# Retention's scores of two token tiles in one stretch, with the delays of TensorE's order set anew

## The chip, the core and the metric

The kernel runs on one core of a Trainium2 chip. The core has five engines that work side by side: TensorE (PE; its weight loads are listed as PEld), VectorE (DVE), ScalarE (ACT), GpSimd (POOL) and SyncE (SP), and queues of DMA transfers. Each engine takes its own instructions in order and waits on semaphores for the others. TensorE writes into PSUM, here eight banks; the other engines read from there. The metric is the time of one execution in microseconds (us), the median over several.

## What is computed

Two layers, each over 1024 tokens of width 1024, with three groups of heads side by side: sliding-window attention (A), retention (B) and gated linear attention, GLA (C). The reference, cut to what matters here:

```python
mod = c_act @ w_mod + b_mod
shift, scale, gate = jnp.split(mod[:, None, :], 3, axis=-1)
h = rms_norm(x, pre_gain) * (1.0 + scale) + shift
proj = h @ w_in                     # columns: aq ak av ag | rq rk rv rg | gq gk gv gg ga
...
r = retention(rq, rk, rv)           # after a rotation of rq and rk
r_out = rms_norm(r) * jax.nn.silu(rg)
...
y = jnp.concatenate([a_out, r_out, g_out], axis=-1) @ w_out
return x + gate * rms_norm(y, post_gain)
```

Retention goes over eight chunks of 128 tokens, four heads of width 64:

```python
def step(state, inp):
    qi, ki, vi = inp
    sc = jnp.einsum('bhid,bhjd->bhij', qi, ki) * dmask
    intra = jnp.einsum('bhij,bhjv->bhiv', sc, vi)
    inter = jnp.einsum('bhid,bhdv->bhiv', qi * q_decay, state)
    new_state = chunk_decay * state + jnp.einsum('bhjd,bhjv->bhdv', ki * k_decay, vi)
    return new_state, intra + inter
```

The state goes from chunk to chunk; the scores `sc` of a chunk need no state.

## The kernel before

**Tiles and projections.** A token tile is 128 tokens, so there are eight tiles and four pairs of them. A projection of one tile to 256 columns is 24 products on TensorE (`accum`, the helper's line L161): eight slices of the width, in three passes, since weights and inputs are split in a high and a low part (L478 makes the low one, L145 and L147 the high one). Retention loops over the pairs: for each of rq, rk and rv it projects the even tile, then the odd one, each into one of three banks `mm`. DVE rotates q and k (L692 to L698) and multiplies them by the decay (L1050) into buffers of the small ring `t1`, which has eight; ACT copies v (L145) into the same ring. The other five banks are `aux`.

**A retention tile.** `ret_core` does for a tile: four transpositions of q and k (L176) into one bank and their copy by ACT (L145); four score products into two banks, one for each half of the 128 rows that a head of width 64 takes; two masks by DVE (L1072); the output's products `po`, for which the state `stR` must be ready; the state's products `pst` and its update by DVE (L1091, L1093). Then come the gate's load (a DMA issued by ACT) and the head norm (L863 to L869). A product of the scores has a shape of 64x128 in the profile and stands there as two instructions.

**What sets the order.** TensorE's order is fixed by the program: code is written out in the order in which TensorE runs it. A planner keeps a clock `clk`, to which each product adds an assumed cost. Everything but the projections is a job, a generator that yields a delay from the table `L` (by `lat(key, l)`; a key ending in `@1` holds for layer 1) or a flag that it must await. Each seven products of a projection `pump` lets those jobs run whose time has come by the planner's clock. So the delays, not the semaphores, say behind which product a transposition or a score stands. The instructions of the other engines are ordered by a scheduler that follows from this, and buffers and banks go round in rings: who asks for the next one waits until the oldest is read.

```python
    def pump():
        moved = True
        while moved:
            moved = False
            for j in list(jobs):
                r = ready(j)
                if r is not None and r <= clk[0]:
                    step(j)
```

**Other places that the table moves.** At the front, input tiles are normalised, transposed (16 transpositions for two tiles, released by DVE's L544, the reader of TensorE being the projection of the tile), split by ACT (L577) and POOL (L581). In the modulation, DVE sums the rows of `w_mod` (L361), TensorE transposes the row and DVE copies it (L273). GLA's scores are 112 small products of a 32x128 shape for each pair of tiles, behind decays by DVE and ACT (L995). L892 takes the GLA gate's projection out of its bank, L807 and L812 are attention's softmax, L1018 writes GLA's masked scores.

## Time and profile before

| | |
|---|---|
| median of 3 runs | 1021.76 us (1021.18 to 1021.92) |
| the profiled execution | 1022.61 us |
| its span in the trace | 1020.9 us |
| mean granted clock of TensorE | 0.978 |
| instructions of TensorE in the trace | 7185 |

The profile's page lists the busy time of each engine as a share of the span, then the span in 40 equal slices, where a digit is the busy share in tenths and the row PEclk is the clock that TensorE was granted, in tenths of full speed. The chain is the work that ended last, followed back from the end: at each step to what released it. A row of the order of time reads: start, duration, engine, line, operation, output<-input, shape, count, and in brackets the idle time ahead of it with its releaser. Rows of one kind that follow each other are put together, so that the start is the first one's. Matmuls overlap, so the time that a product takes is read from the distance between starts. A row of a window reads: the stretch, its length, busy time and count of PE, PEld, DVE, ACT and POOL, the clock, the DMA share and the GB/s.

The layers take about half the span each: retention of layer 0 lies at 110 to 210, GLA's scores of layer 0 at 250 to 370, retention of layer 1 at 600 to 700, GLA's of layer 1 from 718.

### The profile page before, as it was taken

Reading aid. Unit: us, or ns where it says so; the run is one execution under the profiler, and the core shown is the slowest. Engines: PE = TensorE matmul, PEld = TensorE weight load, DVE = VectorE, ACT = ScalarE, POOL = GpSimd, SP = SyncE. Lnnn points to the kernel's source line nnn. Section 1 sums busy time; section 2 is a strip of 40 time slices with the busy share of each in tenths; the row PEclk is TensorE's granted clock in tenths of the full one; section 3 lists DMA queues with packets and bytes.
Section 4 is the critical chain, followed back from the end, with each engine's and each line's share of the span. In section 5 each row is a group of like instructions: output and inputs, shape, how many; then the busy total and the mean of one; then the engine's idle time right before and its main releaser. Section 6 shows DMA issues by size and latency. Waiting matters only on the chain.

```text
span 1020.9 us, 19368 instructions
## 1 busy us (share of the span) xinstructions
PE 975.0 (96%) x7185; PEld 845.1 (83%) x7185; DVE 652.3 (64%) x1565; ACT 377.2 (37%) x1050; POOL 284.5 (28%) x310
## 2 busy tenths in 40 slices
PE   5899999999999999999999999999999999999997
PEld 1588899888998777777888999988899887777886
DVE  3699856766757688754477486676575566763322
ACT  2466321322321556631354342123232256562111
POOL 2343101423331154520235120133243224542000
PEclk8899999999899999999999999999998999999999
DMA  8941613423334245768636142234032214455653
GB/s 292 309 129 47 182 57 104 131 86 109 91 94 141 74 124 164 244 190 268 218 134 202 48 147 71 60 114 138 22 105 86 94 51 134 148 153 185 227 185 144
DMA packets 124153, 140.44 MB, mean 138 GB/s; under 512 B 12462, under 2 KB 95384, under 8 KB 124060
## 3 DMA queue, kind: packets, MB, share of 16 engines
q1 hardware_dynamic: 116060, 127.50, 40.3%
q10 hardware_dynamic: 8000, 11.72, 3.2%
q8 instruction: 56, 0.92, 0.4%
q14 instruction: 37, 0.30, 0.1%
HBM read 102.48 MB, written 34.60 MB: 134 GB/s over the span
## 4 chain that ended last, share of the span: by engine, by line
PE 67%; DVE 13%; DMA 7%; issue 4%; ACT 3%; POOL 1%; SPq 1%; DVEq 0%; POOLq 0%; ACTq 0%
PE mm L161 52%; PE aux L161 11%; PE aux L176 4%; DMA st<-in_w_mod_dram 3%; DVE arena L478 1%; DVE acc L361 1%; DMA t<-t 1%; POOL sm L514 1%; DVE t L573 1%; ACT smx L812 1%; SPq L150 1%; DMA st<-in_w_out_dram 1%; DMA mx<-mixS 1%; DVE t L1050 1%; DVE smx L807 0%
## 5 line engine op out<-in xcount | busy, mean ns | idle before, releaser
L161 PE MATMUL mm<-arena 128*128 128x256 f32 (+2 forms) x1824 | 298.2, 319 | 5.4 <-ACT arena L577 3.0
L161 PE MATMUL mm<-arena,arena 128*128 128x256 f32 (+2 forms) x1824 | 294.3, 318 | 5.0 <-ACT sm L892 2.5
L161 PEld LDWEIGHTS mm<-arena 128*128 128x128 f32 x1824 | 258.5, 193 | 27.3 <-ACT arena L577 3.2
L161 PEld LDWEIGHTS mm<-arena,arena 128*128 128x128 f32 x1824 | 257.3, 192 | 28.2 <-ACT sm L892 3.0
L161 PE MATMUL mm<-arena,mx 128*128 128x512 f32 (+1 forms) x816 | 180.2, 380 | 0.1
L161 PEld LDWEIGHTS mm<-arena,mx 128*128 128x128 f32 x816 | 146.0, 188 | 30.4 <-issue 1.2
L514 POOL TENSOR_TENSOR sm<-sm,mhalf 128x1 f32<-128x1 f32 (+1 forms) x64 | 54.2, 847 | 324.7 <-DVE sm L513 311.8
L478 POOL TENSOR_TENSOR arena<-st,arena 128x512 fp32r<-128x512 f32 x66 | 96.3, 1470 | 94.9 <-ACT arena L145 72.1
L145 ACT ACTIVATE t<-aux 128x512 f32<-128x512 f32 (+1 forms) x96 | 49.2, 522 | 114.3 <-PE aux L176 49.5
L816 POOL TENSOR_TENSOR smx<-smx,sm 128x512 f32<-128x512 f32 x32 | 35.2, 1100 | 112.9 <-DVE sm L815 109.1
L478 DVE TENSOR_TENSOR arena<-st,arena 128x512 fp32r<-128x512 f32 x62 | 60.5, 987 | 7.3 <-ACT arena L145 5.4
L361 DVE SCALAR_TENSOR_TENSOR acc<-st,c_act,acc 128x512 f32<-128x512 f32 x60 | 48.0, 799 | 23.1 <-DMA st<-in_w_mod_dram 22.5
L145 ACT ACTIVATE arena<-st 128x512 fp32r<-128x512 f32 x90 | 52.3, 624 | 20.5 <-PE mm L161 10.9
L812 ACT ACTIVATE smx<-smx,sm 128x129 f32<-128x129 f32 x128 | 50.0, 394 | 20.9 <-DVE sm L809 20.9
L176 PE MATMUL aux<-c_ident,t 128*128 128x128 f32 x288 | 47.2, 288 | 8.0 <-DVE t L544 4.1
L1105 ACT ACTIVATE t<-mm 128x512 f32<-128x512 f32 x30 | 17.9, 596 | 95.8 <-PE mm L161 45.8
L1106 DVE TENSOR_TENSOR t<-mm,modg 128x512 f32<-128x512 f32 x30 | 20.7, 689 | 49.8 <-ACT t L1105 48.6
L176 PEld LDWEIGHTS aux<-c_ident,t 128*128 128x128 f32 x288 | 34.9, 146 | 14.5 <-DVE t L544 5.9
L161 PEld LDWEIGHTS aux<-t,mx 32*128 32x128 f32 (+1 forms) x896 | 43.0, 200 | 4.5 <-DVE sm L273 1.4
L161 PE MATMUL aux<-t,mx 32*128 32x32 f32 (+1 forms) x896 | 44.2, 283 | 2.1 <-DVE sm L273 1.3
L1141 DVE SCALAR_TENSOR_TENSOR t<-t,sm,t 128x512 f32<-128x512 f32 x32 | 23.3, 752 | 35.2 <-DMA t<-xs 19.3
L863 ACT ACTIVATE t<-aux 128x256 f32<-128x256 f32 x32 | 12.3, 384 | 73.8 <-PE aux L161 65.1
(191 smaller groups left out, 1243.0 us busy)
## 6 DMA issues: line engine op xcount, KB each, us to landing
st<-in_w_in_dram SPq DMA_DIRECT2D x96, 256.0 KB, 3.7
st<-in_w_mod_dram SPq DMA_DIRECT2D x64, 256.0 KB, 2.6
mx<-mixS SPq DMA_DIRECT2D x32, 512.0 KB, 5.4
mixS<-t SPq DMA_DIRECT2D x64, 128.0 KB, 2.5
st<-in_w_out_dram SPq DMA_DIRECT2D x32, 256.0 KB, 3.1
mixS<-t SPq DMA_DIRECT2D x32, 256.0 KB, 2.4
wm<-in_w_mod_dram SPq DMA_DIRECT2D x12, 512.0 KB, 7.2
t<-in_x_dram SPq DMA_DIRECT2D x24, 256.0 KB, 4.6
```

The costliest lines, as they stand in the source:

```text
L145: A.activation(dst, src, AF.Copy)
L161: T.matmul(dst, lhsT, rhs, start=start, stop=stop)
L176: T.transpose(dst, src, idn)
L361: V.scalar_tensor_tensor(acc, wt, c_act[:, k:k + 1], acc, ALU.mult, ALU.add)
L478: (G if first == 0 else eng(f"wlo{kc}")).tensor_tensor(wt[:, 1, 2 * kc:2 * kc + 2, 0:256], st, f(hi), ALU.subtract)
L514: G.tensor_tensor(r, r, mhalf[:, :w], ALU.pow)
L812: A.activation(sm[:, h, :], sm[:, h, :], AF.Exp, bias=mx[:, h:h + 1], accum_out=sums[:, h:h + 1])
L816: eng("pn").tensor_tensor(sm[:, :, 0:128], sm[:, :, 0:128], rs.unsqueeze(2).to_broadcast((P, 4, P)), ALU.mult)
L863: A.activation(sq, po, AF.Square)
L1105: A.activation(yg, pm, AF.Square, accum_out=ss[:, nh:nh + 1])
L1106: V.tensor_tensor(yg, pm, modg[l][:, 512 * nh:512 * nh + 512], ALU.mult)
L1141: V.scalar_tensor_tensor(xt[j], yg[j], r, xt[j], ALU.mult, ALU.add)
```

## The change

`ret_core` is taken apart. `ret_turn`, a job for each tile, makes the transpositions and their copy. `ret_core` is now one job for a pair: it starts when both tiles are turned and both have their v, makes the eight score products of the two tiles in one stretch, into the same two banks (tile i in columns 256 i on), then the four masks (L1081 in the changed file), and then for each tile the output's products, the state's products and the state's update (L1102, L1104). `ret_out`, again a job for each tile, loads the gate and does the head norm. Each of the eight products costs the planner 0.112 us where one cost 0.213 by its default. The table `L` has new values nearly throughout. The number of instructions stays the same on TensorE; each kind of work is there as often as before.

```diff
@@ -1050,51 +1050,65 @@
         eng("rdec").tensor_tensor(h4(r), h4(r), dec_.unsqueeze(2).to_broadcast((P, 4, 64)), ALU.mult)
         return r
 
-    def ret_core(l, t, q, k, v):
+    def ret_turn(l, t, q, k):
         yield lat("rc1", l)
         pt = aux()
         for j in range(2):
             transp(pt[:, j * P:(j + 1) * P], q[:, j * P:(j + 1) * P], ident)
             transp(pt[:, (2 + j) * P:(3 + j) * P], k[:, j * P:(j + 1) * P], ident)
         tt_ = t2()
-        qT = tt_[:, 0:256]
-        kTt = tt_[:, 256:512]
         copy("rT", tt_, pt)
-        yield lat("rc2", l)
+        turned[(l, t)] = tt_
+        flag(("rT", l, t), lat("rc2", l))
+
+    turned = {}
+
+    def ret_core(l, p, ks, vs):
+        ts = (2 * p, 2 * p + 1)
+        for t in ts:
+            yield (0.0, ("rT", l, t))
+        qT = [turned[(l, t)][:, 0:256] for t in ts]
+        kT = [turned[(l, t)][:, 256:512] for t in ts]
         sp = [aux(), aux()]
-        for h in range(4):
-            r = slice(64 * (h % 2), 64 * (h % 2) + 64)
-            c = slice((h // 2) * P, (h // 2) * P + P)
-            mult(sp[h % 2][:, c], kTt[r, c], qT[r, c], True, True)
-        sc = t2()
-        scv = h4(sc)
-        for c in range(2):
-            V.tensor_tensor(scv[:, c:4:2], sp[c][:, 0:256].rearrange("p (h q) -> p h q", h=2),
-                            causal.unsqueeze(1).to_broadcast((P, 2, P)), ALU.mult)
+        for i in range(2):
+            for h in range(4):
+                r = slice(64 * (h % 2), 64 * (h % 2) + 64)
+                c = slice((h // 2) * P, (h // 2) * P + P)
+                mult(sp[h % 2][:, 256 * i + c.start:256 * i + c.stop], kT[i][r, c], qT[i][r, c], True, True, 0.112)
+        sc = [t2(), t2()]
+        for i in range(2):
+            for c in range(2):
+                V.tensor_tensor(h4(sc[i])[:, c:4:2], sp[c][:, 256 * i:256 * i + 256].rearrange("p (h q) -> p h q", h=2),
+                                causal.unsqueeze(1).to_broadcast((P, 2, P)), ALU.mult)
         yield lat("rc3", l)
-        if t > 0:
-            yield (0.0, ("stR", l, t))
-        po = aux()
-        for j in range(2):
+        for i, t in enumerate(ts):
             if t > 0:
-                mult(po[:, j * P:(j + 1) * P], qT[:, j * P:(j + 1) * P], stR[:, j, :], True, False)
-            for h in (2 * j, 2 * j + 1):
-                mult(po[:, 64 * h:64 * h + 64], sc[:, h * P:(h + 1) * P], v[:, 64 * h:64 * h + 64],
-                     t == 0, t == 0 or h % 2 == 1)
-        if t < NT - 1:
-            pst = aux()
+                yield (0.0, ("stR", l, t))
+            po = aux()
             for j in range(2):
-                mult(pst[:, j * P:(j + 1) * P], k[:, j * P:(j + 1) * P], v[:, j * P:(j + 1) * P], True, True)
-            for c in range(2):
-                r = slice(64 * c, 64 * c + 64)
-                blk = stR[r, :, 64 * c:64 * c + 64]
-                V.tensor_tensor(blk, blk, pst[r, 0:256].rearrange("p (j n) -> p j n", j=2)[:, :, 64 * c:64 * c + 64],
-                                ALU.add)
-            V.tensor_tensor(stR, stR, cdt.unsqueeze(2).to_broadcast((P, 2, P)), ALU.mult)
-            flag(("stR", l, t + 1), lat("rc4", l))
+                if t > 0:
+                    mult(po[:, j * P:(j + 1) * P], qT[i][:, j * P:(j + 1) * P], stR[:, j, :], True, False)
+                for h in (2 * j, 2 * j + 1):
+                    mult(po[:, 64 * h:64 * h + 64], sc[i][:, h * P:(h + 1) * P], vs[i][:, 64 * h:64 * h + 64],
+                         t == 0, t == 0 or h % 2 == 1)
+            if t < NT - 1:
+                pst = aux()
+                for j in range(2):
+                    mult(pst[:, j * P:(j + 1) * P], ks[i][:, j * P:(j + 1) * P], vs[i][:, j * P:(j + 1) * P],
+                         True, True)
+                for c in range(2):
+                    r = slice(64 * c, 64 * c + 64)
+                    blk = stR[r, :, 64 * c:64 * c + 64]
+                    V.tensor_tensor(blk, blk, pst[r, 0:256].rearrange("p (j n) -> p j n", j=2)[:, :, 64 * c:64 * c + 64],
+                                    ALU.add)
+                V.tensor_tensor(stR, stR, cdt.unsqueeze(2).to_broadcast((P, 2, P)), ALU.mult)
+                flag(("stR", l, t + 1), lat("rc4", l))
+            job(ret_out(l, t, po[:, 0:256]))
+
+    def ret_out(l, t, po):
         sg = t1()
         dma("lsr", sg, srS[t])
-        yield from head_norm_gate(l, t, po[:, 0:256], sg, 4.0 / 64.0, 4.0 * EPS, 4)
+        yield from head_norm_gate(l, t, po, sg, 4.0 / 64.0, 4.0 * EPS, 4)
 
 
     def y_half(l, t, nh, mixt, ss, yg):
@@ -1203,7 +1217,10 @@
                     if name == "rv":
                         v = t1()
                         copy("rv", v, src)
-                        job(ret_core(l, t, rr[("rq", tt)], rr[("rk", tt)], v))
+                        rr[("rv", tt)] = v
+                        job(ret_turn(l, t, rr[("rq", tt)], rr[("rk", tt)]))
+                        if tt:
+                            job(ret_core(l, p, [rr[("rk", i)] for i in range(2)], [rr[("rv", i)] for i in range(2)]))
                     else:
                         rr[(name, tt)] = ret_rot(t, src, qdec if name == "rq" else kdec)
                     pump()
...
-"rc1": 0.8, "rc2": 1.47, "rc3": 1.99, "rc4": 2.79, "fin1": 10.74, "lay1": 1.23,
+"rc1": 0.05, "rc2": 1.52, "rc3": 1.31, "rc4": 2.31, "fin1": 7.77, "lay1": 1.23,
...
```

What the table does to the order is seen in four places. In the rows the number behind a name tells one buffer from another, and differs between the two kernels for the same thing. The first is TensorE at the front, with the projections of tiles 0 and 1 (`mm_410` to `mm_556`) and tile 2's first product (`mm_617` before, `mm_614` now). Before:

```order
L161 MATMUL mm_410<-arena_71 128x272 x24
L161 MATMUL mm_444<-arena_71 128x272 x21
L176 MATMUL aux_466<-c_ident,t_53_319 128x128 x4
L176 MATMUL aux_478<-c_ident,t_54_320 128x128 x4
L176 MATMUL aux_490<-c_ident,t_58_331 128x128 x4
L176 MATMUL aux_502<-c_ident,t_59_332 128x128 x4
L161 MATMUL mm_444<-arena_71 128x272 x3
L161 MATMUL mm_526<-arena_318,arena_71 128x256 x24
L161 MATMUL mm_556<-arena_318,arena_71 128x256 x24
L176 MATMUL aux_598<-c_ident,sm_442 16x128
L161 MATMUL mm_617<-arena_71 128x272 x24
```

and now:

```order
L161 MATMUL mm_410<-arena_71 128x272 x24
L161 MATMUL mm_444<-arena_71 128x272 x24
L161 MATMUL mm_478<-arena_318,arena_71 128x256 x24
L161 MATMUL mm_508<-arena_318,arena_71 128x256 x7
L176 MATMUL aux_516<-c_ident,t_53_319 128x128 x4
L176 MATMUL aux_528<-c_ident,t_54_320 128x128 x4
L176 MATMUL aux_540<-c_ident,t_58_331 128x128 x4
L176 MATMUL aux_552<-c_ident,t_59_332 128x128 x4
L161 MATMUL mm_508<-arena_318,arena_71 128x256 x17
L176 MATMUL aux_615<-c_ident,sm_442 16x128
L161 MATMUL mm_614<-arena_71 128x272 x24
```

The 16 transpositions of tiles 2 and 3 have moved behind 34 more products; between them and tile 2's first product there were 51, and are 17.

The second is TensorE at the last pair of retention in layer 0: transpositions, then score products (`aux`<-`t` of 128x128, alternating between two banks), then the output's products, which read `stR`. Of rows that repeat in turn only the first ones are shown. Before (the even tile's):

```order
L161 MATMUL mm_2404<-arena_318 128x256 x7
...
L176 MATMUL aux_2424<-c_ident,t_389_2194 128x128
L176 MATMUL aux_2424<-c_ident,t_409_2306 128x128
...
L161 MATMUL mm_2404<-arena_318 128x256 x14
L161 MATMUL aux_2445<-t_432_2429 128x128
L161 MATMUL aux_2446<-t_432_2429 128x128
...
L161 MATMUL mm_2404<-arena_318 128x256 x3
L161 MATMUL mm_2480<-arena_71,arena_318 128x512 x4
...
L161 MATMUL aux_2499<-stR,t_432_2429 128x128
```

and now (the odd tile's transpositions, the scores of both tiles, the even tile's output):

```order
L161 MATMUL mm_2465<-arena_71,arena_318 128x512 x4
L176 MATMUL aux_2470<-c_ident,t_387_2222 128x128
L176 MATMUL aux_2470<-c_ident,t_407_2334 128x128
...
L161 MATMUL mm_2465<-arena_71,arena_318 128x512 x8
L161 MATMUL aux_2488<-t_422_2411 128x128
L161 MATMUL aux_2489<-t_422_2411 128x128
...
L161 MATMUL aux_2488<-t_436_2475 128x128
L161 MATMUL aux_2489<-t_436_2475 128x128
...
L161 MATMUL mm_2465<-arena_71,arena_318 128x512 x8
L161 MATMUL aux_2512<-stR,t_422_2411 128x128
```

The scores stood 14 products of 256 columns behind their transpositions and stand now 8 of 512 columns behind the later ones; and the output's products followed the scores after 3 of 256, 8 of 512 and four transpositions, now after 8 of 512.

The third is TensorE ahead of the first GLA scores of layer 0, where `rows` is the modulation's row that DVE's L273 copies and that the decayed q and k need. Before:

```order
L161 MATMUL mm_2873<-arena_71 128x256 x17
L161 MATMUL mm_2924<-arena_318 128x512 x12
L176 MATMUL aux_2977<-c_ident,rows_2882 128x16
L161 MATMUL mm_2924<-arena_318 128x512 x8
L176 MATMUL aux_2993<-c_ident,t_504_2865 128x128 x2
L176 MATMUL aux_3002<-c_ident,mx_2476 128x128 x2
L161 MATMUL aux_3007<-t_517_2933,mx_2476 128x32
```

and now:

```order
L161 MATMUL mm_2850<-arena_71 128x256 x7
...
L176 MATMUL aux_2865<-c_ident,rows_2808 128x16
L161 MATMUL mm_2850<-arena_71 128x256 x17
...
L161 MATMUL mm_2924<-arena_318 128x512 x20
L176 MATMUL aux_2988<-c_ident,mx_2461 128x128 x2
L161 MATMUL aux_2993<-t_514_2936,mx_2461 128x32
```

The row's transposition has moved ahead of 17 products of 256 and 20 of 512 columns.

The fourth is DVE in layer 1, at the rotation of k of the second pair's odd tile: L692 to L698 and L1050 write it, L1102 and L865 to L869 belong to the pair before. What a row waits for stands in brackets, with a number for the semaphore. Before:

```order
L692 TENSOR_TENSOR t1_1339_7506<-mm_1333_7468,sincos_95 128x256 [waits PE_49]
L694 TENSOR_TENSOR t1_1340_7507<-mm_1333_7468,sincos_95 128x4x32
L695 TENSOR_TENSOR t1_1340_7507<-mm_1333_7468,sincos_95 128x4x32
L697 TENSOR_TENSOR t1_1338_7505<-t1_1339_7506,t1_1340_7507 128x4x32 [waits DMAHW5_49,DVE_49]
L698 TENSOR_TENSOR t1_1338_7505<-t1_1339_7506,t1_1340_7507 128x4x32 [waits DVE_49]
L1050 TENSOR_TENSOR t1_1338_7505<-t1_1338_7505,c_kdec_387 128x256 [waits DVE_49]
```

and now:

```order
L692 TENSOR_TENSOR t1_1318_7459<-mm_1316_7433,sincos_95 128x256 [waits PE_49]
L694 TENSOR_TENSOR t1_1319_7460<-mm_1316_7433,sincos_95 128x4x32
L695 TENSOR_TENSOR t1_1319_7460<-mm_1316_7433,sincos_95 128x4x32
L697 TENSOR_TENSOR t1_1317_7458<-t1_1318_7459,t1_1319_7460 128x4x32 [waits DVE_49,PE_49]
L698 TENSOR_TENSOR t1_1317_7458<-t1_1318_7459,t1_1319_7460 128x4x32 [waits DVE_49]
L1102 TENSOR_TENSOR stR_391<-stR_391,aux_1325_7512 64x2x64
L1050 TENSOR_TENSOR t1_1317_7458<-t1_1317_7458,c_kdec_387 128x256 [waits DVE_49]
```

L697 waits now for TensorE as well: for the state's products of the pair before, `aux_1325_7512`, which read the last of its buffers; those stand on TensorE behind 31 products that follow the projection `mm_7433`.

2 lines of the change are left out of this document (1 added, 1 removed).

## The prediction

> **What bounds the kernel now.** I read the busy shares and the clock first, then the chain that ended last, then the waits of TensorE (PE) by what they waited for, and at the places that the change touches the order of time.
>
> ```profile
> PE 975.0 (96%) x7185; PEld 845.1 (83%) x7185; DVE 652.3 (64%) x1565; ACT 377.2 (37%) x1050; POOL 284.5 (28%) x310
> ...
> PEclk8899999999899999999999999999998999999999
> ...
> PE 67%; DVE 13%; DMA 7%; issue 4%; ACT 3%; POOL 1%; SPq 1%; DVEq 0%; POOLq 0%; ACTq 0%
> ```
>
> TensorE works 975.0 of 1020.9 us, and the chain lies on it for two thirds. So time is won or lost in three ways: TensorE's own work per product, its gaps (some 46 us in all), and the slices whose granted clock is below 9 tenths. The gaps of this kind, over the whole span (total, times, longest):
>
> ```profile
> PE mm L161 <- ACT sm L892: 4.2, 3, 1.7
> ...
> PE aux L176 <- DVE smx L807: 2.8, 3, 1.7
> PE aux L176 <- DVE mx L1018: 2.6, 5, 0.6
> ```
>
> These are small waits, spread over the projections of the gates (L892), attention (L807) and the gated linear attention (GLA, L1018). Retention's own come below.
>
> **The change, part 1: one stretch of eight score products for two of four.** TensorE around one stretch of before, and 14 products of 256 columns elsewhere; the rows of 124.40, 124.62 and 124.73 cut the same eight instructions (two for each product) at different starts:
>
> ```profile
> 124.19 0.28 PE L161 MATMUL mm<-arena,arena 128*128 128x256 f32 x1
> 124.40 0.72 PE L161 MATMUL aux<-t 64*128 64x128 f32 x8
> ...
> 124.62 0.50 PE L161 MATMUL aux<-t 64*128 64x128 f32 x6
> ...
> 124.73 0.39 PE L161 MATMUL aux<-t 64*128 64x128 f32 x4
> ...
> 125.05 1.90 PE L161 MATMUL mm<-arena,arena 128*128 128x256 f32 x14
> 126.88 0.69 PE L161 MATMUL aux<-gaT,gwt 32*128 32x512 f32 x1
> ...
> 137.79 1.92 PE L161 MATMUL mm<-arena 128*128 128x256 f32 x14
> 139.54 0.49 PE L176 MATMUL aux<-c_ident,t 128*128 128x128 f32 x3
> ```
>
> By the starts, an ordinary product takes (139.54 - 137.79)/14 = 0.125. The stretch takes 125.05 - 124.40 = 0.65, the product ahead of it 0.21 (0.085 more than 0.125), and the 14 behind it 1.83 in place of 1.75 (0.08 more). With its two edges one stretch costs 0.815. Inside, two instructions (one product) go by in 124.73 - 124.62 = 0.11. The longer stretch adds four products at 0.11 = 0.44 and drops one whole stretch, so a pair of tiles saves 0.815 - 0.44 = 0.375, and eight pairs (four in each layer) **3.0 us**. Were the added products each to cost a quarter of the stretch, 0.16, only 0.17 a pair or 1.3 us would stay: the two ends are 1.3 and 3.0, and I take 3.0, because the 0.11 is measured inside the stretch and the 0.65 holds a change of kind at its end.
>
> [...]
>
> **Part 2: retention's waits.** Transposes become a job of their own, ahead of the scores; the scores come a good deal later. TensorE's waits in 110 to 210 (layer 0) and in 660 to 700 (layer 1), then what lies behind the longest:
>
> ```profile
> PE aux L161 <- ACT t L145: 2.2, 2, 1.7
> PE aux L161 <- DVE t L1072: 1.0, 1, 1.0
> ...
> PE aux L176 <- DVE t L1050: 0.7, 1, 0.7
> ...
> PE aux L161 <- ACT t L145: 1.8, 1, 1.8
> PE aux L176 <- DVE t L1050: 0.7, 1, 0.7
> PE aux L161 <- DVE t L1072: 0.6, 1, 0.6
> ```
> ```profile
> 199.95 0.38 ACT L145 ACTIVATE t<-mm 128x256 f32<-128x256 f32 x1 [4.69 <-DVE t L698]
> ...
> 201.15 0.72 PE L161 MATMUL aux<-t 64*128 64x128 f32 x8 [1.71 <-ACT t L145]
> ...
> 202.25 1.08 PE L161 MATMUL mm<-arena,arena 128*128 128x512 f32 x4
> 203.17 0.60 PE L176 MATMUL aux<-c_ident,t 128*128 128x128 f32 x4
> 203.52 1.17 PE L161 MATMUL mm<-arena,arena 128*128 128x512 f32 x4
> ...
> 205.87 0.77 PE L161 MATMUL aux<-t,t 128*128 128x64 f32 x4 [0.96 <-DVE t L1072]
> ```
>
> They sum to 7.0. Four of them go away by the new order. The 2.2 and the 1.8 (scores ahead of the copy of the transposes, which ACT held back 4.69 us because a buffer of the small ring came free late) have now more products between: before, 14 of 0.125 = 1.75 us; after, in layer 0's last pair eight of 512 columns at (203.17 - 202.25)/4 = 0.23 = 1.84 us behind the *odd* tile's transposes, and in layer 1's last pair twenty = 4.6 us. The 0.6 of layer 1 goes since its masks have now 24 products of 256 or 12 of 512 columns (2.8 to 3.0 us) ahead of their readers in every pair, and the 0.7 since the last pair's odd transposes stand 17 x 0.125 + 4 x 0.23 = 3.0 us behind the products ahead of them. Those four are 5.3. At layer 0's last pair the cover hardly grows, and between the stretch and its first reader stand now eight products, 1.84 us, where 201.79 to 204.53 was 2.7: its 1.0 can grow by up to 0.9. I take 5.3 less 1.1 for that growth and for a rest of the copy's wait: **4.2 us**, ends 7.0 (all gone) and nothing.
>
> **Part 3: GLA's first stretch.** The table moves the transposition of the rows, which stood eight products of 512 columns (1.8 us) ahead of its reader, ahead of 17 of 256 and 20 of 512 (6.7 us). TensorE at that place, the chain of waits over it and over the first stretch of layer 1, and windows (span, busy time with counts of PE, PEld, DVE, ACT, POOL, then clock, DMA):
>
> ```profile
> 250.83 0.40 PE L161 MATMUL aux<-t,mx 32*128 32x32 f32 x2 [1.31 <-DVE sm L273]
> 251.89 1.48 PE L161 MATMUL aux<-t,mx 32*128 32x32 f32 x28 [0.65 <-ACT t L995]
> ...
> 251.89 6.50 PE aux L161 x122
> ...
> 718.99 3.67 PE aux L161 x122
> ...
> 248.80:252.20 3.40, 1.43 (x22) 1.04 (x20) 3.34 (x10) 2.11 (x5) 0.83 (x1) 1.00 0.14 30
> 252.20:262.40 10.20, 10.20 (x134) 9.58 (x130) 4.45 (x10) 3.19 (x9) 1.89 (x3) 0.50 0.48 148
> 757.40:760.80 3.40, 3.40 (x114) 3.23 (x114) 3.40 (x13) 1.50 (x4) 0.90 (x2) 1.00 0.02 5
> 760.80:767.60 6.80, 6.53 (x54) 6.17 (x51) 4.00 (x14) 2.21 (x8) 1.99 (x5) 0.50 0.24 80
> ```
>
> After a window in which TensorE worked 1.43 of 3.40 us the clock is 0.50 for 10.2 us, three windows of 3.4; the 122 small products take 6.50 where they take 3.67 at full clock. With the rows read early the 1.31 goes. A window at half clock costs at most 3.4/2 = 1.7; one fewer of the three makes **1.31 + 1.7 = 3.0 us**. Ends: 1.31 + 2 x 1.7 = 4.7, and nothing, when another input of the stretch is late in its place.
>
> [...]
>
> **Part 4: the front.** The sixteen transposes of input tiles 2 and 3 go behind 34 more products (34 x 0.125 = 4.2 us), which takes them off their wait of 0.76, but only 17 products (2.1 us) are left until tile 2's first product, which had 51 (6.1 us).
>
> ```profile
> 52.23 1.09 PE L176 MATMUL aux<-c_ident,t 128*128 128x128 f32 x8 [0.76 <-DVE t L544]
> ...
> 60.93 1.27 PE L161 MATMUL mm<-arena 128*128 128x272 f32 x8 [1.67 <-ACT sm L892]
> ...
> 58.36 1.28 POOL L581 TENSOR_TENSOR arena<-t,arena 128x512 fp32r<-128x512 f32 x1 [1.29 <-ACT arena L577]
> ...
> 75.00:90.00 15.00, 13.96 (x113) 13.39 (x111) 15.00 (x36) 7.60 (x21) 3.70 (x3) 1.00 0.08 27
> ```
>
> At best 0.76 + 1.67 = 2.4 is won. At worst the tiles' low halves, whose last POOL instruction ends at 59.64, 7.4 us behind the transposes of 52.23, end up behind their reader: TensorE starts them 4.2 - 0.76 = 3.4 later, and reaches the reader sooner by the 0.5 that is left of its wait, so up to 2.9 is lost. DVE is busy 15.00 of 15.00 right behind, so that work which comes earlier meets a full engine there. I take **0**.
>
> **Part 5: what the change adds.** A pair's odd tile keeps its k and v in the ring of eight small buffers until its state product. In layer 1 of the new order DVE's rotary (L697) and ACT's copy of rv (L145) of the *next* pair wait for that product, in three of the four pairs; before, no such wait stands there. DVE waits for it in order: behind it stand L698, the state update, the decay (L1050) and the head norm. From the end of the projection that L697 belongs to, TensorE runs 24 + 7 products (3.9 us) and about 0.7 of state products (eight at the 0.35/4 of 203.17 to 203.52); DVE has 1.0 us of work in it, so it stands 3.6 us in each, 10.8 in three. Is there room?
>
> ```profile
> 660.00:685.00 25.00, 24.16 (x211) 23.42 (x210) 16.98 (x45) 6.54 (x14) 7.21 (x6) 1.00 0.39 110
> 685.00:697.00 12.00, 9.52 (x72) 8.18 (x71) 10.56 (x24) 4.19 (x9) 3.39 (x4) 1.00 0.81 234
> ```
>
> DVE is free 8.0 us in the first window and 1.4 in the second. Two of the standstills (7.2) fit in the first, the third not: 3.6 - 1.4 = 2.2 reach TensorE. The ends are 0 (the next transposes come 24 products or 3.0 us later) and 10.8. I add three new waits of the mean size of the eight of L807 and L1018, (2.8 + 2.6)/8 = 0.7, for the delays set anew elsewhere: together **+4.3 us**. Instruction counts do not change, so no DMA or queue work is added; the gate's load stays on ACT's queue and lies now in a later job.
>
> **Sum.** -3.0 - 4.2 - 3.0 + 0 + 4.3 = -5.9. The profiled execution took 1022.61, so 1016.7 there; it lies 0.85 over the median of the runs, 1021.76, which gives 1015.9.
>
> **Rivals.** *The gain is dealt out again* (within 0.2%, or 2.04 us, about what a measurement of this kernel tells from no change): nothing won at GLA because another input is late (+3.0), and masks that wait for the doubled stretch (+0.9 to 1.5): 1015.9 + 4.2 = 1020.1. For it speaks that ACT's t L995 was late by 0.65 right behind the rows. *The ring stalls DVE* (slower): all 10.8 reach TensorE, 8.6 more than in the sum: 1024.5. It decides where over 2.0 + 5.9 + 2.2 = 10.1 of the 10.8 reach it; against it speaks DVE's free third in 660 to 685. Together with the front's 2.9 it needs 7.2. *The clock* (slower): the stretches of small products fall differently against the windows, and six more windows go at half clock: 6 x 1.7 = 10.2, which is 1026; that the fall came behind a fully busy window too makes the number of windows a matter of chance, two of them more or less being likely (3.4 us). *Nothing of it reaches the end:* against this, TensorE is busy nine tenths in nearly every slice to the last, so what it is spared in the middle stays.
>
> **How the numbers follow.** Forecast 0.68, faster by over 0.2%, with its own range 1009 to 1019.7; dealt out again 0.14, within 0.2%; the ring 0.10 and the clock 0.08, slower. The range goes from 1009.5 (the forecast with both GLA windows, the front's gain and a free ring: -1.7 - 2.4 - 2.2) up to 1024.5, the ring's time; about 2 in 10 stay outside.
>
> **What the profile after would show.** Eight stretches of sixteen instructions of about 1.1 to 1.3 us in place of sixteen of 0.65; no wait for ACT t L145 over 1 us at the scores; no wait for L273 ahead of GLA's first stretch and at most two half-clock windows there; DVE standing some 3 us at L697 in layer 1 released by PE. A wait of TensorE for L1081 or for L1050 beyond 1 us, a new wait ahead of tile 2's first product near 58, or over ten windows at half clock would make it wrong.

## The result, and the profile after

The changed kernel takes 1012.09 us (median of 5 runs, 1006.8 to 1013.59) and the kernel before, in runs beside it, 1021.18 us (1019.25 to 1021.92): a ratio of 0.9906 with a 95% interval of 0.9878 to 0.9935. It is faster by 9.1 us; 5.9 were forecast, 1015.9 us with a range of 1009.5 to 1024.5. The profiled execution of the changed kernel took 1013.59 us with a span of 1011.7, the slowest of its five, at a mean clock of 0.971 where before had 0.978.

The page of the changed kernel, its busy shares, its granted clock and its chain:

```profile
PE 972.2 (96%) x7185; PEld 845.3 (84%) x7185; DVE 653.4 (65%) x1565; ACT 377.4 (37%) x1050; POOL 279.7 (28%) x310
...
PEclk8899999999899999999999999999988999999999
...
PE 78%; DVE 10%; DMA 5%; ACT 3%; issue 3%; POOL 1%; SPq 0%; ACTq 0%; DVEq 0%; POOLq 0%
```

TensorE is idle for 1011.7 - 972.2 = 39.5 us where it was 45.9. So of the 9.2 us between the two spans 6.4 are waits and 2.8 are busy time, although more of the busy time was spent at half clock. The waits of TensorE over the whole span, after:

```profile
PE mm L161 <- DVE t L882: 4.0, 2, 2.1
...
PE aux L176 <- DVE mx L1018: 2.9, 6, 0.6
PE mm L161 <- ACT sm L892: 2.5, 1, 2.5
...
PE aux L161 <- ACT t L145: 2.0, 1, 2.0
PE aux L176 <- DVE smx L807: 1.3, 2, 0.8
...
PE aux L161 <- DVE t L1081: 0.6, 1, 0.6
```

Against the rows of before, the waits for ACT's copy (L145) went from 4.0 to 2.0, those for the masks (now L1081) from 1.5 to 0.6, attention's (L807) from 2.8 to 1.3, and those for the decay (L1050) and the rows (L273) are gone. L882, at the front, is up from 0.7 to 4.0. Not every difference belongs to the change: in a second trace of the changed kernel (below) TensorE is idle for 36.7 us, L882 stands at 2.7 and the masks have no wait.

For what follows two numbers are worked out for each run: its span times the mean clock, and the rest of the span. The first is what the span would be if every product took twice as long at half clock; the second is then what the clock cost. Not every product does: in the trace of the changed kernel 14 products of 256 columns take 3.14 us at half clock (110.80 to 113.94) and 1.78 at full (180.63 to 182.41), 1.76 times as long. So the second is an upper bound, but the two help to tell apart what an edit did to the work and the waits from what it did to the clock. Medians of each kernel's runs, the ratios against runs of the kernel before in the same session; two slow executions, of 1198.55 us (pairs, old delays, old cost) and 2423.03 us (two stretches, rest in place), are left out:

| kernel | us | ratio, 95% interval | span x clock | rest |
|---|---|---|---|---|
| before (61 runs) | 1022.2 | | 997.1 | 23.5 |
| the changed kernel, first session | 1012.09 | 0.9906 (0.9878 to 0.9935) | 981.9 | 27.3 |
| the changed kernel again | 1010.92 | 0.9888 (0.9866 to 0.9910) | 982.2 | 26.2 |
| pairs, old delays | 1026.53 | 1.0058 (1.0037 to 1.0080) | 996.3 | 28.7 |
| pairs, old delays, old cost | 1016.97 | 0.9948 (0.9926 to 0.9969) | 991.4 | 23.4 |
| old core, new delays | 1024.70 | 1.0020 (0.9999 to 1.0040) | 994.1 | 29.6 |
| before, rows early | 1036.48 | 1.0159 (1.0133 to 1.0185) | 1002.9 | 33.1 |
| two stretches | 1022.33 | 1.0004 (0.9990 to 1.0017) | 992.1 | 28.6 |
| two stretches, rest in place | 1012.30 | 0.9890 (0.9869 to 0.9912) | 985.5 | 23.3 |
| longer turn | 1015.58 | 0.9931 (0.9907 to 0.9955) | 985.5 | 27.9 |
| changed, wide GLA products | 998.95 | 0.9770 (0.9741 to 0.9800) | 986.3 | 10.5 |
| before, wide GLA products | 1014.16 | 0.9911 (0.9891 to 0.9930) | 1000.7 | 11.6 |
| GLA halves | 1035.12 | 1.0127 (1.0084 to 1.0169) | 997.5 | 37.2 |
| GLA halves in layer 1 | 1012.64 | 0.9903 (0.9872 to 0.9934) | 986.8 | 24.3 |

By it the change won 15 us of work and waits, and 3 to 4 went back to the clock.

### The profile page after: what moved, and what is told of

It reads as the page before. It is cut to its first block, busy times and chain, and to the rows that moved or that the text cites. A ratio compares the mean times of both kernels' runs of the same rounds, so it can differ in the third digit from the quotient of the medians.

```text
span 1011.7 us, 19347 instructions
## 1 busy us (share of the span) xinstructions
PE 972.2 (96%) x7185; PEld 845.3 (84%) x7185; DVE 653.4 (65%) x1565; ACT 377.4 (37%) x1050; POOL 279.7 (28%) x310
## 4 chain that ended last, share of the span: by engine, by line
PE 78%; DVE 10%; DMA 5%; ACT 3%; issue 3%; POOL 1%; SPq 0%; ACTq 0%; DVEq 0%; POOLq 0%
PE mm L161 61%; PE aux L161 12%; PE aux L176 4%; DMA st<-in_w_mod_dram 1%; DVE t L573 1%; DVE arena L478 1%; ACT smx L812 1%; POOL sm L514 1%; DMA mixS<-t 1%; DMA xk<-in_x_dram 1%; DMA t<-t 1%; DVE t L544 1%; DVE acc L361 0%; DMA c_freq<-cst_freq_dram 0%; DVE arena L147 0%
## 5 line engine op out<-in xcount | busy, mean ns | idle before, releaser
L161 PE MATMUL mm<-arena,arena 128*128 128x256 f32 (+2 forms) x1824 | 299.9, 320 | 7.1 <-DVE t L882 4.0
L161 PEld LDWEIGHTS mm<-arena 128*128 128x128 f32 x1824 | 260.7, 195 | 27.9 <-ACT arena L577 3.2
L145 ACT ACTIVATE t<-aux 128x512 f32<-128x512 f32 (+1 forms) x96 | 48.4, 519 | 91.2 <-PE aux L161 49.1
L145 ACT ACTIVATE arena<-st 128x512 fp32r<-128x512 f32 x90 | 52.5, 624 | 27.3 <-PE mm L161 13.8
L361 DVE SCALAR_TENSOR_TENSOR acc<-st,c_act,acc 128x512 f32<-128x512 f32 x60 | 48.2, 803 | 14.4 <-DMA st<-in_w_mod_dram 13.4
L145 ACT ACTIVATE t<-mm 128x256 f32<-128x256 f32 x40 | 14.9, 379 | 73.6 <-PE mm L161 30.6
L161 PEld LDWEIGHTS aux<-t,mx 32*128 32x128 f32 (+1 forms) x896 | 39.7, 188 | 2.1 <-issue 1.2
L161 PE MATMUL aux<-t,mx 32*128 32x32 f32 (+1 forms) x896 | 40.6, 272 | 0.0
```

The source lines that it names most:

```text
L145: A.activation(dst, src, AF.Copy)
L161: T.matmul(dst, lhsT, rhs, start=start, stop=stop)
L361: V.scalar_tensor_tensor(acc, wt, c_act[:, k:k + 1], acc, ALU.mult, ALU.add)
```

## The experiments

**Each part alone.** The first question is whether the terms of the sum are really terms: the pairs with the old table, and the old core with the new one.

```diff
 # pairs, old delays: the changed kernel with
-L = {"tt1": 6.37, "tt2": 5.87, "tb1": 24.85, ...
+L = {"tt1": 6.37, "tt2": 6.45, "tb1": 24.5, ...
 # old core, new delays: the kernel before with the opposite
```

> The new structure (one stretch of eight scores per pair, transposes and output as jobs of their own) with the old table of delays. Theory 1 (each part carries its own term): the stretches give their 3.0 us and little else, since with the old delays the scores stand close behind the copy and GLA's rows stay late: 1018 to 1019, retention's wait for ACT's copy stays or grows. Rival (the table does all of it, the stretch is worth nothing by itself): 1021 or more.

> The old structure (four scores per tile) with the new table. Theory 1: GLA's first stretch loses its 1.3 us wait for the rows, and waits of retention and attention change; the 3.0 us of the stretches are missing: 1014 to 1017. Rival (the table fits only the new structure): 1020 or more, with new waits in retention.

Neither part gains: 1026.53 us is 4.5 more than the kernel before beside it (1022.04), and 1024.70 is 2.7 more, though the interval of its ratio still takes in 1. Both expectations of theory 1 missed, and both times are those of the rivals. The waits of the first, and then of the second, whole span:

```profile
PE aux L176 <- DVE t L544: 8.9, 4, 3.8
...
PE aux L161 <- ACT t L995: 4.8, 2, 3.4
```
```profile
PE aux L176 <- DVE mx L1018: 7.6, 7, 4.3
...
PE mm L161 <- DVE t L695: 3.0, 1, 3.0
```

The largest waits are mostly not in retention: L544 is the normalisation ahead of a layer, L995 and L1018 are GLA's. The planner's clock says behind which product a job stands; the pair's eight products at 0.112 where eight at 0.213 were move it by 8 x 0.101 = 0.8 for each pair, and with it what is timed by the table afterwards. So one more run gives the pairs the old cost again:

```diff
-                mult(sp[h % 2][...], kT[i][r, c], qT[i][r, c], True, True, 0.112)
+                mult(sp[h % 2][...], kT[i][r, c], qT[i][r, c], True, True)
```

> The new structure with the old delays, as in the first run (1026.5), but with the planner's old cost for each score product, so that its clock goes on as in the kernel before and less of the order behind retention moves (1030 of 6243 products stand elsewhere than before, not 1710; none in the stretch from a third to a half of the program, where the first run moved 234). Theory A (the loss of the first run came from the delays fitting no longer, not from the pairs): the stretches' 3 us show, 1018 to 1021, with fewer waits for L544 and L995 and 994 us or less by span times mean clock. Rival (the pairs themselves cost time with scores so close behind the copy): 1025 or more, with waits in retention.

It takes 1016.97 us, 5.2 less than before beside it (1022.12), a little under the 1018 to 1021 of theory A: the rival falls, and the pairs are worth some 5 us once most of the order stays where its delays were made for. That is 2 more than the stretches' 3.0, and 1030 products still stand elsewhere than before, so not all of it need be the pairs' own. The loss of 4.5 came with the planner's cost. One thing that is left against the new table can be seen in retention. TensorE's waits in 110 to 215 and in 595 to 712 of this run:

```profile
PE aux L161 <- DVE t L1081: 2.2, 1, 2.2
...
PE aux L161 <- DVE t L1081: 2.3, 1, 2.3
```

These are waits for masks, 4.5 us in all, at the third pair of each layer; in the trace of the changed kernel 0.6 remain, at the third pair of layer 0. The new table doesn't win this by more distance from the scores to their readers. At that pair 24 products stand between here (175.17 to 178.14, 2.97 us) and 14 in the changed kernel (180.63 to 182.41, 1.78 us). What differs is what stands on DVE ahead of the masks. DVE there, layer 0, then layer 1:

```profile
177.25 1.72 DVE L361 SCALAR_TENSOR_TENSOR acc<-st,c_act,acc 128x512 f32<-128x512 f32 x1 [1.52 <-DMA st<-in_w_mod_dram]
178.89 1.48 DVE L1050 TENSOR_TENSOR t<-t,c_qdec 128x256 f32<-128x256 f32 x1
180.30 1.40 DVE L1081 TENSOR_TENSOR t<-aux,c_causal 128x256 f32<-128x256 f32 x4
...
661.49 1.66 DVE L361 SCALAR_TENSOR_TENSOR acc<-st,c_act,acc 128x512 f32<-128x512 f32 x1 [2.10 <-DMA st<-in_w_mod_dram]
```

The masks stand behind a sum of the modulation that waits 1.52 or 2.10 for its DMA and then takes 1.7 where one at 173.85 takes 0.75, and behind a decay of 1.48. They start 5.1 us after the stretch's end; in the changed kernel they start 2.3 after it, at 182.90.

**The stretch itself.** TensorE around one pair of layer 1 in the changed kernel:

```profile
639.94 1.16 PE L161 MATMUL aux<-t 64*128 64x128 f32 x16
641.03 0.63 PE L161 MATMUL mm<-arena,arena 128*128 128x256 f32 x3
```

The stretch takes 641.03 - 639.94 = 1.09, as the prediction had it (0.65 + 0.44). To see what a second stretch costs, it is cut again, in two ways:

```diff
         for i in range(2):
+            if i:
+                yield 0.2
             for h in range(4):
 # "rest in place" besides: rc3 1.31 -> 0.62, in layer 1 2.37 -> 1.75
```

> The changed kernel with the eight scores split again in two stretches of four, with seven ordinary products or more between them; all else as it is. Theory 1 (a stretch costs its two changes of kind): 0.375 us for each of eight pairs, 3.0 us slower than the changed kernel, about 1015. Rival (the products' number counts, not the stretches'): no change, 1012.

> The changed kernel with each stretch of eight scores cut in two of four by three to seven ordinary products, as in the run before it with two stretches, but with rc3 shortened by what the cut adds to the planner's clock, so that nearly all else stands where the changed kernel has it (86 of 6243 products stand elsewhere). Theory A (a stretch costs its two changes of kind, and the 10 us of the first run with two stretches came from all that moved behind it): 0.375 us for each of eight pairs, 3 us more than the changed kernel, 1013 to 1015, waits and half-clock windows about as there. Rival (two stretches by themselves cost the 10 us): 1020 or more.

The first cut cost 10 us (1022.33), more than either theory gave. With its waits

```profile
PE aux L176 <- DVE mx L1018: 7.2, 6, 4.3
...
PE mm L161 <- ACT sm L892: 5.8, 2, 3.3
```

it is the same case as above: what stands behind a cut moved. With that taken out, 1012.30, a little under the 1013 to 1015 of theory A. The same pair there:

```profile
638.12 0.72 PE L161 MATMUL aux<-t 64*128 64x128 f32 x8
638.76 0.62 PE L161 MATMUL mm<-arena,arena 128*128 128x256 f32 x3
639.31 0.71 PE L161 MATMUL aux<-t 64*128 64x128 f32 x8
639.96 2.75 PE L161 MATMUL mm<-arena 128*128 128x256 f32 x21
```

From the start of the first stretch to the end of the second 639.96 - 638.12 = 1.84, less three ordinary products of 0.125: 1.465. The whole stretch takes 1.09, so a cut costs 0.375 at this pair, the forecast amount; eight make 3.0. In span times clock the run is 3.3 to 3.6 behind the changed kernel. In the time itself it is not seen: the two ratios, 0.9890 and 0.9888, are as good as equal, with half-widths of 0.0022, since this run lost 3 to 4 us less to the clock. That the stretch gives 3 us is shown in the trace, and not in the median.

**The wait that stayed.** At the last pair of layer 0 the changed kernel still stops. TensorE, then ACT, at that place:

```profile
204.36 0.71 PE L161 MATMUL aux<-t 64*128 64x128 f32 x8
207.10 0.71 PE L161 MATMUL aux<-t 64*128 64x128 f32 x8 [2.03 <-ACT t L145]
...
202.99 0.63 ACT L145 ACTIVATE arena<-st 128x512 fp32r<-128x512 f32 x1 [2.51 <-DMA st<-in_w_in_dram]
...
205.00 0.63 ACT L145 ACTIVATE arena<-st 128x512 fp32r<-128x512 f32 x1 [1.10 <-DMA st<-in_w_in_dram]
...
206.46 0.60 ACT L145 ACTIVATE t<-aux 128x512 f32<-128x512 f32 x1
```

The stretch breaks in its middle, since the odd tile's copy (206.46) stands on ACT behind casts of weights that wait for their DMA. Moving the scores further away tells whether distance helps:

```diff
-"rc2": 1.52,
+"rc2": 3.46,
```

> The changed kernel with one delay, rc2 of layer 0, at layer 1's 3.46 in place of 1.52, so that scores stand further behind their transposes. Theory 1: the wait of 2.0 us for ACT's copy at layer 0's last pair is gone, 1010. Rival (ACT is held up by casts of weights that wait for their DMA, so that the wait moves to the masks or the output): 1012 or more.

The wait for the copy is gone and the stretch stands whole, as theory 1 had it, but the kernel is some 4 us slower than the changed one, the time of the rival: the masks have a wait of 1.5 now in 110 to 230 (at the third pair, not at the last one), and GLA behind it waits longer, 7.4 for L1018 where it was 2.9.

```profile
PE aux L161 <- DVE t L1081: 1.5, 1, 1.5
...
PE aux L176 <- DVE mx L1018: 7.4, 6, 4.3
```

**The rows and GLA's first stretch.** The two delays that put the row's transposition early, alone in the kernel before:

```diff
-"mod5": 3.36, "mod6": 5.14,
+"mod5": 0.27, "mod6": 2.31,
```

> The kernel before with two delays of the modulation alone taken from the new table (mod5 and mod6 of layer 0), which moves the rows' transposition ahead. Theory 1: the wait for DVE's copy of the rows (1.3 us) is gone and one half-clock window fewer follows (1.7 us): 1018. Rival (another input of the stretch is late in its place, the clock falls all the same): 1021, and 10 us at half clock behind 250 stay.

Both theories missed: 1036.48 us, 14.4 more than before. TensorE in GLA there, the rows with a wait:

```profile
235.61 0.28 PE L176 MATMUL aux<-c_ident,rows 16*128 16x16 f32 x1 [4.09 <-DVE mx L1018]
...
276.70 1.41 PE L161 MATMUL aux<-t,mx 32*128 32x32 f32 x41 [2.50 <-ACT t L995]
300.20 1.41 PE L161 MATMUL aux<-t,mx 32*128 32x32 f32 x41 [1.40 <-ACT t L995]
```

The wait for L273 is not among its waits any more. In its place a transposition stands where L1018 holds it up for 4.09, and two later stretches wait for L995. By the table 5.8 of the loss are work and waits, and at most 9.6 the clock.

**The clock.** The clock was half in GLA whether or not a wait stood ahead: at 252.20 in the kernel before, behind a window with TensorE busy for 1.43 of 3.40 us, and at 233.70 in the changed kernel, behind one with 3.40 of 3.40. To see whether the small products do it, they are left out: 16 products of 128x128 for each pair stand in their place (the scores are then not the reference's), in the changed kernel and in the one before.

```diff
         for c in range(2):
-            for s in range(1, 4):
...
+            for g2 in range(2):
+                for h in range(4):
+                    w = kxz[:, h % 3, c] if g2 else kds[h][:, P * c:P * c + P]
+                    x = ad if h % 2 else q1
+                    mult(sp[h][:, ...], w, x[:, P * c:P * c + P], True, True, 0.189)
```

> GLA's small score products left out and, in their place, 16 products of 128x128 for each pair, which take about as long (3.4 to 4 us) and wait for the same inputs; the scores are not the reference's. Theory 1 (small products pull the clock down): no half-clock window in 228 to 310 and 700 to 780, where the changed kernel had nine or ten; 1012 less up to 15 plus 8 x 0.6 for longer stretches: 998 to 1004. Rival (waits or TensorE's changes of kind pull it down): the windows stay, 1012 to 1018.

> The kernel before with GLA's small score products left out and 16 products of 128x128 for each pair in their place, as was done to the changed kernel (999); the scores are not the reference's. Theory A (the change won more in waits and in TensorE's work than it shows, and gave a part of it back as half-clock windows in GLA): 1009 to 1013, so that the two kernels without those windows lie 10 to 14 us apart. Rival (the clock took as much from both): 1008, as far apart as the two kernels are.

The stretch 222 to 322 (layer 0's GLA) as windows, of the changed kernel and then of the one before, both with wide products; the clock is the number behind POOL's count:

```profile
222.00:322.00 100.00, 99.37 (x775) 92.41 (x774) 74.98 (x212) 30.79 (x87) 32.99 (x47) 1.00 0.40 119
```
```profile
222.00:322.00 100.00, 97.05 (x744) 89.79 (x744) 71.15 (x204) 28.83 (x84) 32.15 (x44) 0.98 0.35 105
```

In the changed kernel the half-clock windows of GLA are all gone, and the time is 998.95, 12 to 13 less. So in this kernel GLA's half-clock windows go with the small products: nine with them, none without. The wide products also drop TensorE's changes of kind, but those alone don't do it: "two stretches, rest in place" has sixteen stretches of 64-row products in retention, and TensorE is at full clock over both of them:

```profile
64.50:252.00 187.50, 181.27 (x1606) 169.33 (x1605) 141.43 (x376) 65.88 (x154) 43.97 (x47) 1.00 0.33 103
300.00:712.90 412.90, 409.58 (x2836) 356.92 (x2834) 279.18 (x645) 162.72 (x459) 117.95 (x120) 1.00 0.47 145
```

Without the small products the kernel before takes 1014.16, 1 us over what theory A gave it. By the ratios the two kernels lie 0.9911 - 0.9770, or 14.4 us, apart without them and 9.6 to 11.4 with them: some 3 to 5 us of what the change won seem to have gone back to the clock in GLA, about as the rest of the span says. Each of these ratios is only known to 2 or 3 us, so the amount is an estimate. The trace of the changed kernel with its small products shows how, in windows before and behind a stretch, once in each layer:

```profile
230.30:233.70 3.40, 3.40 (x124) 3.36 (x127) 1.54 (x3) 0.45 (x2) 0.55 (x2) 1.00 0.71 205
233.70:237.10 3.40, 3.40 (x23) 2.62 (x17) 2.47 (x7) 0.93 (x4) 0.73 (x2) 0.50 0.36 114
...
708.20:711.60 3.40, 3.40 (x128) 3.24 (x124) 0.27 (x1) 1.61 (x5) 0.81 (x3) 1.00 0.00 0
711.60:715.00 3.40, 2.88 (x9) 1.61 (x6) 2.16 (x6) 0.70 (x4) 0.47 (x1) 0.50 0.02 5
```

A window full of small products (some 125 instructions) is followed by one at half clock, though TensorE is not idle in it. Was this a matter of one run? The changed kernel was run once more:

```diff
 # no edit
```

> The changed kernel once more, for its spread and for a trace of another run. Theory of the clock (stretches of small products pull the clock down where they fill a window of 3.4 us of a grid that runs by itself): the half-clock windows lie elsewhere or are of another number than in the first trace, with a time of 1007 to 1014 that goes with the time at half clock. Rival (waits pull it down): the same windows at the same places.

In GLA its half-clock windows lie at the same stretches (234, 254, 275, 295, 708, 729, 749 and twice at 770). Of the others the ones at 111 and 544 are missing and one at 207 is new. Over the eleven runs the time goes roughly with the clock: 1006.8 us at 0.977, 1013.59 at 0.971, though one at 0.977 took 1011.69. So the places in GLA are those that the rival gave, but not by its cause, since no wait stands ahead of the falls at 234 and 712. The stray ones do go with waits: at 111 and 544 the first trace has waits of 2.1 (L882) and 2.2 (L1132), the second 0.8 and none.

Last, GLA's stretch in two halves of 28 products each (the trace counts two instructions for a product, so the 112 named ahead are 56 products), other jobs held back between: in both layers, then in layer 1 alone.

```diff
+        hold[0] = True
         for c in range(2):
+            if c:
+                yield 0.9
...
+        hold[0] = None
 # in pump: only the job that holds is stepped
 # in layer 1 alone: "if c and l", and gc3 of layer 1 0.86 -> 3.0
```

> The changed kernel with GLA's stretch of small products cut in two halves of 1.65 us, with some 14 ordinary products of 256 or 8 of 512 columns (1.8 us) between; other jobs are held back meanwhile. Theory 1: no window of 3.4 us is filled by small products any more, most of the nine or ten half-clock windows go, at up to 1.7 us each, and eight more changes of kind cost 8 x 0.2: 1000 to 1006. Rival (the clock falls for another reason): the windows stay and the time is 1014 or more.

> GLA's stretch of small products in two halves in layer 1 alone, with the delay ahead of the transposes of its masked scores (gc3 of layer 1) longer by 2.1, since in the run with halves in both layers the clock fell behind waits, and in layer 1 only behind the waits for those transposes. Theory A (the clock falls behind a window of 3.4 us in which TensorE is busy with full products for less than about 0.4 of it, by a wait or by small products): no half-clock window or one in 700 to 790, where the changed kernel had five, 1005 to 1008. Rival (halves spoil the clock by themselves, as a mix of kinds): five windows or more, 1014 or more.

The first is 23 to 24 us slower than the changed kernel, with the most clock lost of all (37.2), where theory 1 gave 1000 to 1006: in its trace GLA has eleven windows at half clock in layer 0 and three in layer 1, where the changed kernel has four and five. The second has the changed kernel's time, 1012.64, but a wide spread: 1006.15 us in a run with a clock of 0.985 and 1018.65 in one with 0.968. In its trace the clock fell three times in layer 1, for five windows in all (one each at 711 and 728, three at 769), as many as in the changed kernel, so theory A missed. Two of the falls came behind these rows of TensorE:

```profile
725.80 1.38 PE L162 MATMUL aux<-t,mx 32*128 32x32 f32 x41 [0.54 <-DVE t L873]
...
767.66 1.38 PE L162 MATMUL aux<-t,mx 32*128 32x32 f32 x41 [0.74 <-DVE t L873]
```

With a wait of 0.5 or 0.7 for DVE in the half stretch, TensorE is busy with other products for 0.26 and 0.27 of these two windows, and half clock followed, as it did behind the whole stretches of the changed kernel, where that share was 0.07 to 0.19. No version that computes the reference's scores beats the changed kernel beyond its interval.

## Why the prediction was right, and where it was not

The direction and the range held, and 9.1 us were won where 5.9 were forecast. Its steps held less well than its sum: TensorE's waits fell by some 5 us more than forecast and the clock took 3 to 4 where 1.7 was to be won, and that these two lie on opposite sides is luck.

- **Part 1, the stretches, -3.0:** right in mechanism and size: 1.09 us for a stretch, 0.375 for a cut.
- **Part 2, retention's waits, -4.2:** right in sum, and partly by luck, since its misses offset each other. Of 7.0 us there remain 2.0 for the copy, 0.6 for the masks and 0.4 for the state, so 4.0 went. One of the four that were to go did not: the wait for ACT's copy at layer 0's last pair grew from 1.7 to 2.0, since I counted the products between and not the casts on ACT that wait for DMA. The masks' 1.0 at that pair was to grow by up to 0.9 and is gone, in "longer turn", where the stretch stands whole, too. The 0.6 is another wait, at the third pair, where 14 products stand between:

```profile
183.37 0.76 PE L161 MATMUL aux<-t,t 128*128 128x64 f32 x4 [0.58 <-DVE t L1081]
```

  In layer 1 all are gone, 3.1 us.
- **Part 3, GLA's first stretch, -3.0:** the 1.3 went, and behind that stretch one window at half clock is left of three. But the term took one stretch and left the others out: they now fall one by one, nine windows in GLA in the place of eight, so the 1.7 for the clock was not won.
- **Part 4, the front, 0:** mis-sized. TensorE's waits from 45 to 115, before and after:

```profile
PE mm L161 <- ACT sm L892: 3.1, 2, 1.7
PE aux L176 <- DVE t L544: 0.8, 1, 0.8
PE mm L161 <- DVE t L882: 0.7, 1, 0.7
PE mm L161 <- DVE arena L581: 0.4, 1, 0.4
```
```profile
PE mm L161 <- DVE t L882: 4.0, 2, 2.1
PE mm L161 <- ACT sm L892: 2.5, 1, 2.5
PE mm L161 <- POOL arena L581: 0.8, 1, 0.8
```

  5.0 became 7.3, a loss of 2.3, near the upper end of 2.9; in the second trace it is 6.0, a loss of 1.0. The wait for L892 that was to go stands ahead of tile 2's first product at 59 and is longer, 2.5 where it was 1.7. Two windows at half clock followed in the first trace (at 60 and 111), one in the second, and none before.
- **Part 5, new waits, +4.3:** the step that failed. DVE does stand at L697 in layer 1, as the order said; the three places after:

```profile
631.67 0.29 DVE L697 TENSOR_TENSOR t<-t,t 128x128 f32<-128x128 f32 x1 [3.35 <-PE aux L161]
...
644.40 0.29 DVE L697 TENSOR_TENSOR t<-t,t 128x128 f32<-128x128 f32 x1 [1.13 <-PE aux L176]
...
654.87 0.29 DVE L697 TENSOR_TENSOR t<-t,t 128x128 f32<-128x128 f32 x1 [1.09 <-PE aux L161]
```

  One is 3.35 of the 3.6 expected, the others about 1.1 (the middle one released by a transposition), and nothing of them reaches TensorE, which from 595 to 705 waits for no one. The 2.2 was charged for work with slack behind it: behind the standstill of 3.35 the k is done at 632.68, and the next transpositions stand at 634.75, 2.1 us later. Nor did the three other new waits, charged at 2.1, come: attention's and the second layer's went down, and the one that grew, at L1132 from 1.1 to 2.2, is missing in the second trace. TensorE's idle time fell by 6.4 (1.6 of it is a wait for a DMA of `w_mod` at the start, which comes and goes between runs), where the terms for waits (-4.2, -1.3, +4.3) make 1.2.
- **The rivals.** The ring that stalls DVE: the wait is there, its price is nothing. The clock: it took part, as a loss of 3 to 4 us by the rest of the span and of some 3 to 5 by the wide products, not the 10.2 that would have turned the sign. More than ten windows at half clock were to make the prediction wrong; behind the first 45 us there are twelve, where before has eight, and the gain was larger all the same. Masks behind the doubled stretch: 0.6 us with the new delays, where before has 1.5 behind the single ones, and 4.5 with the old delays and the old cost, where DVE's sums that wait for DMA stand ahead of them.
- **What the sum hid.** It added the stretch, the waits and the rows as if each could be had alone. The pairs with the old table cost 4.5 and the old core with the new one 2.7 (at the edge of its interval); with both, 9 to 11 are won. Of the 14.7 us between the spans of the two traces without GLA's small products, TensorE's idle time explains 8.3 (43.4 and 35.1 by their spans and busy times) and the stretches 3.0. The rest, 3.4, is busy time; at most 1.7 of it is one window more at half clock in the kernel before (three and two), and where the remainder comes from stays open.

## What to carry to other kernels

A table of planned delays belongs to the order for which it was made: an edit that moves the planner's clock is to be measured with the planner's cost kept as it was first, and with the delays set anew second, or its own worth is not seen. For each wait that the new order is to remove, ask what the releasing engine does in order ahead of the release (here ACT's casts and DVE's sums, which waited 1.1 to 2.5 us for DMA), not only how many products lie between. Where the time of a kernel goes with the granted clock (here 1006.8 us at 0.977 and 1013.59 at 0.971), compare edits by span times mean clock beside the median.

## What the runs showed of the hardware

From 45 to 1005 us the granted clock falls to 0.50 five times in the trace of before and eleven times in that of the changed kernel; what follows is what TensorE did in the 3.4 us ahead of each. Of the eleven falls, three (at 60, 111 and 544) stand behind a window with a wait of TensorE and without small products, busy for 0.28, 0.39 and 0.36 of it. The first two of them, each with the window behind it:

```profile
56.20:59.60 3.40, 0.94 (x8) 0.66 (x8) 3.40 (x9) 2.95 (x10) 1.26 (x1) 1.00 0.11 39
59.60:63.00 3.40, 3.40 (x18) 3.40 (x17) 3.40 (x8) 3.40 (x11) 2.35 (x2) 0.51 0.56 161
107.40:110.80 3.40, 1.33 (x12) 1.14 (x11) 2.15 (x3) 1.69 (x5) 2.40 (x2) 1.00 0.04 14
110.80:114.20 3.40, 3.40 (x16) 3.34 (x17) 3.40 (x11) 0.00 (x0) 0.00 (x0) 0.51 0.75 201
```

The other eight stand in GLA, behind windows in which TensorE is busy for 0.98 to 1.00, but for only 0.07 to 0.19 with products other than GLA's of 32 rows (230.30 and 708.20 above are two of them). In the kernel before, that share is 0.11, 0.41, 0.30, 0.13 and 0.35 ahead of the five falls. The window at 736.89 there has a share of 0.34 and full clock behind it, so that the share alone doesn't tell every fall. What it is in the small products that goes with a fall (rows, columns or length), no run here tells.

Cutting GLA's stretch in halves gave no fewer windows at half clock: in both layers fourteen in place of nine, in layer 1 alone five there as in the changed kernel, and there two of the three falls came behind a half stretch with a wait of its own (0.54 and 0.74 us).
